# Paced convolution steps and the end of the final RMSNorm, in a two-layer decoder trunk on one core

## The chip, the core and the metric

The kernel runs on one NeuronCore of a Trainium2 chip. Five engines work side by side, each with its own in-order queue: TensorE (PE) multiplies matrices, VectorE (DVE), ScalarE (ACT) and GpSimd (POOL) do elementwise work, and SyncE (SP) issues most of the DMA transfers. They wait for one another by semaphores. The metric is the time of one execution on the device, in microseconds (us).

## The reference

Input x is 512 tokens of 1024 channels, float32; the output has the same shape. There are two layers and a final norm:

```python
h = h + conformer_conv(rmsnorm(h), ...)    # layer A
h = h + swiglu_ffn(rmsnorm(h), ...)
k, v = split(rmsnorm(h, norm_kv) @ w_kv)   # once
h = h + banded_sink_attention(rmsnorm(h) @ w_q, k, v, ...) @ w_o   # layer B
h = h + swiglu_ffn(rmsnorm(h), ...)
out = rmsnorm(h, norm_final)

def conformer_conv(x, ...):
    a = glu(x @ w_pw1 + b_pw1)
    y = causal depthwise conv of a, width 31, + b_dw
    y = silu(layernorm(y))                  # over the channels
    return y @ w_pw2 + b_pw2

def swiglu_ffn(x, w_up, w_down):            # width 2816
    gate, up = split(x @ w_up)
    return (silu(gate) * up) @ w_down
```

rmsnorm(x, g) is x * rsqrt(mean(x*x) + 1e-6) * g, the mean over the channels.

## The kernel before

**Layout.** Everything is transposed: channels lie on the 128 partitions, tokens on the free axis. h is eight tiles of 128 x 512. Where it helps, tokens are worked in two halves of 256 (HALF[0], HALF[1]); h0 and h1, and fa and fb, are objects of the first and the second half.

**Products in three parts.** Most products go through mm3: weight and activation are each split into a high and a low part, and PE computes high by high (L262), weight-high by activation-low (L263) and weight-low by activation-high (L264). The first half's second pointwise product (pw2) is the exception, with one plain matmul (L260). Weights come as a stream of 128 x 1024 chunks in a fixed plan. SP loads them (L187) up to six chunks ahead; up to three chunks ahead ACT casts the high part (L203) and DVE subtracts it from the raw chunk for the low part (L204). `get` hands out the next chunk, and is the clock of all pacing.

**The background convolution.** The depthwise convolution of the first half, h0, is done before its pw2. That of the second half, h1, is a generator of 85 steps, 20 of which are taken early; the other 65 are recorded between the weight chunks of the first half's pw2 (8 chunks), FFN up and FFN down. `job(second, points...)` paces them: at each `get`, `pace` takes steps until as many are done as `due_at` gives by straight lines between the points (chunk, steps done), and behind the last point all the rest. One step works on two channel tiles: per tile one DVE multiply-add (L611), and on average about one product on ACT (L603), which POOL adds up (L604), through a ring of eight `pr` buffers. After each of the four pairs of tiles come its squares (DVE L638, ACT L640) and, on PE with a matrix of ones, its sums (L649). After the last pair follow the LayerNorm's scales: ACT copies the sums (L655), PE turns them (L658), DVE computes mean and variance (L660 to L665), POOL takes a power (L671), ACT makes diagonals (L676), PE spreads them (L680). Then, per channel tile, DVE subtracts and multiplies (L692, L693), ACT applies silu (L694), and the result is split for the second half's pw2 (ACT L386, DVE L387). That pw2 starts when the first half's FFN is over.

**The first half's rows.** As pw2 of the first half yields its eight row tiles, DVE adds each to h (L731). ACT then scales it and casts the high part of the FFN's input (L382), DVE makes the low part (L383), ACT squares (L336) and DVE adds the squares up (L340). The FFN's first matmuls need these parts.

**The end.** The last FFN down product is worked by halves, class Fin: fa, then fb. For each half: `rows` adds PE's result to h (DVE L1047), squares it (ACT L1051) and adds squares (POOL L1053); of fb only the first five tiles are added on POOL. PE turns squares into sums per token with tiny matmuls (`total`, L1039): for fb, in the order tile 5, tile 6, the run of five, tile 7. `sums` computes the mean (`ms`, DVE L1070), the power -1/2 (`rs`, POOL L1072) and a diagonal from it (`diag`, DVE L1074); `spread` broadcasts it with PE (L1084, for fb also into a second bank, L1088, copied by ACT, L1093). The final products are h times the gain times this scale: six tiles of each half on DVE (`out_dve`, L1106, stored by SP, L1096), and two on POOL (`out_pool`, L1100) from tiles that ACT has multiplied by the gain (L1079), stored by SP for fa and by ACT for fb. `fill(n)` places n of fa's DVE products among fb's last steps.

**What sets the order.** The code is recorded once, by tiles; a scheduler then places each engine's instructions by its own estimate of when they can run. `tc.issue_after(x)` keeps what is recorded inside it behind x. So the place of an instruction in an engine's queue need not be the place at which it was recorded.

The last chunks of the kernel, as recorded:

```python
    for n, (kp, g) in enumerate(steps):
        fb.down(kp, g)
        if n == 1:
            fa.sums()
        elif n == 2:
            fb.rows(0)
            fa.spread()
        elif n == 3:
            fb.rows(1, fill)
```

Of the kernel before, what the change touches and what calls it, by code (L numbers as in the profile page):

```python
# [21 lines left out]
KT = D // P  # L22
# [127 lines left out]
def hybrid_trunk(ctx: ExitStack, tc: tile.TileContext, xT, W, prm_in, wdw_in, sinks, relb, onehot, outT):  # L150
    nc = tc.nc
# [10 lines left out]
    def uid(s):  # L162
        ctr[0] += 1
        return f"{s}{ctr[0]}"

    def bank():
        return ps.tile([P, 512], F32, tag="bank", name=uid("bank"))
# [4 lines left out]
    def temp():  # L172
        return tmp.tile([P, 512], F32, tag="tmp", name=uid("tmp"))
# [35 lines left out]
    def job(gen, *points):  # L209

        jobs.append([gen, points, 0])
# [54 lines left out]
    class Act:  # L266
        def __init__(self, n, w=512):
            self.per = 2048 // w
            self.q = [tuple(quads.tile([P, self.per, w], F32R, tag="quad", name=uid("quad")) for _ in range(2))
                      for _ in range(-(-n // self.per))]  # L270
# [51 lines left out]
    def col(name, i):  # L322
        c = PARAM_COLS[name] + i
        return prm[:, c:c + 1]


    class Rms:
# [44 lines left out]
        def spread(self):  # L372
            self.step1()
            pb = bank()[:, 0:self.w]
            self.spread_mm = nc.tensor.matmul(pb, ones_m, self.diag, start=True, stop=True).ins  # L375
            return pb
# [171 lines left out]
    with tc.tile_pool(name="conv", bufs=2) as cv:  # L548
# [29 lines left out]
        class Half:  # L578
# [64 lines left out]
            def sums(self, p):  # L643
                if self.st is None:
                    self.st = bank()
                for e in range(2):
                    ct = 2 * p + e
                    for f, t in enumerate((self.y[:, ct, :], self.sq[e])):
                        mm = nc.tensor.matmul(self.st[:, f * W2:(f + 1) * W2], ones_m, t,  # L649
                                              start=ct == 0 and f == 0, stop=ct == KT - 1 and f == 1)  # L650
                return mm.ins
# [30 lines left out]
            def rows(self, split_z):  # L682
                pb = self.pb
                if split_z:
                    zz = Act(KT, W2)
                    self.z = [zz[i] for i in range(KT)]
                else:
                    zz = quads.tile([P, KT, W2], F32, tag="quad", name=uid("z"))
                    self.z = [zz[:, i, :] for i in range(KT)]
                for i in range(KT):  # L690
                    t = temp()[:, 0:W2] if split_z else self.z[i]
                    nc.vector.tensor_sub(t, self.y[:, i, :], pb[:, 0:W2])  # L692
                    nc.vector.tensor_mul(t, t, pb[:, W2:2 * W2])  # L693
                    self.silu = nc.scalar.activation(t, t, AF.Silu, scale=col("lng", i), bias=col("lnb", i)).ins  # L694
                    if split_z:
                        split(self.z[i], t)
                    yield
# [84 lines left out]
        done, early, late = 0, 0, None  # L782
        for at_, (hf, ct) in enumerate(projs):
# [3 lines left out]
            with tc.issue_after(spread) if at_ == 13 else nullcontext():  # L787
                proj = Pw1(hf, ct, mid=(lambda: h0.sums(3)) if at_ == 11 else None)
# [14 lines left out]
            if at_ == 10:  # L803
                h1 = Half(1, h0.last)
                second = h1.background()
# [15 lines left out]
            late.gate()  # L821
        h1.after = [h0.silu]
        base = seen[0]
        job(second, (base, 0), (base + 8, 20), (base + 36, h1.n_steps - early))
        x0 = {"ffn0": Act(KT)}
        bc0 = new_bc()
        n0 = Next(("ffn0",), x0, bc0, HALF[0], nc.vector)
# [15 lines left out]
    base = seen[0]  # L843
# [15 lines left out]
    if True:  # L859
# [20 lines left out]
        for half in range(2):  # L880
# [7 lines left out]
            if half == 0:  # L888
                rs_bc = rms.step2()
                rs = rms.rs  # L890
                for m in range(2):
                    t = temp()
# [4 lines left out]
        for n in range(4):  # L897
            t = temp()
# [100 lines left out]
        for part in range(2):  # L999
            for g in range(2):  # L1000
# [4 lines left out]
                for m in range(4):  # L1005
                    i = g * 4 + m
# [13 lines left out]
    class Fin:  # L1020
        def __init__(self, hf):
            self.hf, self.tok = hf, HALF[hf]
            self.banks, self.hg = [bank() for _ in range(4)], []
            self.n_pool = 2

        def down(self, kp, g):
            whi, wlo = get("down", 1, kp, g)
# [14 lines left out]
        def rows(self, g, other=lambda n, ins: None):  # L1042

            n_add = 5 if self.hf else KT
            for i in range(g * 4, g * 4 + 4):
                t = h[i][:, self.tok]
                add = nc.vector.tensor_add(t, self.banks[i // 2][:, (i % 2) * 256:(i % 2) * 256 + 256], t)  # L1047
                if i == KT - 1:
                    other(2, add.ins)
                sq = res.tile([P, 256], F32, tag="sq", name=uid("sq"), bufs=5)  # L1050
                self.squared = nc.scalar.square(sq, t).ins  # L1051
                if 0 < i < n_add:
                    nc.gpsimd.tensor_add(sq, self.acc, sq)  # L1053
                if i < n_add:
                    self.run = self.acc = sq
                if not self.hf or i < n_add:
                    continue
                if i == n_add:
                    self.st = bank()
                self.total(sq, i == n_add, i == KT - 1)  # L1060
                if i == KT - 2:
                    self.total(self.run, False, False)

        def sums(self, other=lambda n, ins: None):
            if not self.hf:
                self.st = bank()
                self.total(self.acc, True, True)
            st = self.st
            ms = small.tile([P, 4], F32, tag="ms", name=uid("ms"))
            other(2, nc.vector.tensor_scalar(ms[:, 0:2], st[:, 0:2], 1.0 / D, EPS, op0=ALU.mult, op1=ALU.add).ins)  # L1070
            rs = small.tile([P, 4], F32, tag="rs", name=uid("rs"))
            nc.gpsimd.tensor_tensor(rs[:, 0:2], ms[:, 0:2], mhalf[:, 0:2], op=ALU.pow)  # L1072
            self.diag = temp()[:, 0:256]
            other(2, nc.vector.tensor_mul(self.diag.rearrange("p (n q) -> p n q", n=2),  # L1074
                                          ident.unsqueeze(1).to_broadcast([P, 2, P]),
                                          rs[:, 0:2].unsqueeze(2).to_broadcast([P, 2, P])).ins)
            for i in range(self.n_pool):
                t = res.tile([P, 256], F32, tag="res", name=uid("res"))
                nc.scalar.mul(t, h[i][:, self.tok], col("fin", i))  # L1079
                self.hg.append(t)  # L1080

        def spread(self):
            self.pb = bank()[:, 0:256]
            nc.tensor.matmul(self.pb, ones_m, self.diag, start=True, stop=True)  # L1084
            if self.hf:

                pb = bank()[:, 0:256]
                nc.tensor.matmul(pb, ones_m, self.diag, start=True, stop=True)  # L1088
                self.copy(pb)

        def copy(self, pb):
            self.bc = temp()[:, 0:256]
            nc.scalar.copy(self.bc, pb)  # L1093

        def store(self, i, t, q=nc.sync):
            q.dma_start(outT[i][:, self.tok], t)  # L1096
# [1 line left out]
        def out_pool(self):  # L1098
            for i, t in enumerate(self.hg):
                nc.gpsimd.tensor_mul(t, t, self.bc)  # L1100
                self.store(i, t, nc.scalar if self.hf else nc.sync)

        def out_dve(self):
            for i in range(self.n_pool, KT):
# [3 lines left out]
                self.store(i, t)  # L1108
                yield

    res = ctx.enter_context(tc.tile_pool(name="res", bufs=8))
    steps = [(kp, g) for kp in range(*LAST) for g in range(2)]
    fa = Fin(0)
    for kp, g in steps:
# [3 lines left out]
    fb = Fin(1)  # L1118
# [7 lines left out]
    for n, (kp, g) in enumerate(steps):  # L1126
# [5 lines left out]
            fa.spread()  # L1132
        elif n == 3:
            fb.rows(1, fill)
    with tc.issue_after(fb.squared):
        fa.copy(fa.pb)
    fa.out_pool()
    fb.sums(fill)
    fb.spread()
    for _ in fb.out_dve():  # L1140
# [28 lines left out]
```

## Time and profile before

| | us |
|---|---|
| median of three runs | 1115.81 |
| lowest, highest | 1115.38, 1116.58 |
| profiled execution, its own time | 1115.77 |
| its span in the profile | 1114.0 |
| PE busy in the span | 1098.9 |
| DVE busy | 662.3 |
| ACT busy | 502.6 |
| POOL busy | 322.1 |
| mean granted PE clock | 0.993 of full speed |

The profile has one execution; its times count from the start of its span. Most views are lists: a timeline row is start, duration, engine, line of the kernel, operation, output<-inputs, shape, and "xN" where N like instructions are merged into one row; in brackets stands how long the engine stood idle ahead of it, and what ended that. A row by stretches has the busy time of PE, PE's weight loads, DVE, ACT and POOL in the stretch (each with its number of instructions), then PE's granted clock (1.00 is full speed), the busy share of the DMA engines, and GB/s. The ends of matmuls are modelled, so merged PE rows overlap their neighbours somewhat.

### The profile page before, as it was taken

What the parts mean: (1) busy time and instruction counts of PE and PEld (TensorE: products, weight loads), DVE (VectorE), ACT (ScalarE), POOL (GpSimd) and SP (SyncE); (2) the same over time, 40 slices, a digit from 0 to 9 for tenths busy, and PEclk for the clock granted to TensorE, in tenths of its full rate; (3) what the DMA queues carried; (4) which work ended last, traced back from release to release, by engine and by line L of the source; (5) the groups of instructions that cost most, each with busy time, mean ns of one, the idle gap of its engine ahead of it and who ended that gap; (6) DMA issues with size and microseconds to landing.
All of it is one profiled execution on the core that took longest, in us unless ns stands there. A gap on an engine that the chain in (4) does not pass through costs nothing.

```text
span 1114.0 us, 15803 instructions
## 1 busy us (share of the span) xinstructions
PE 1098.9 (99%) x5994; PEld 955.7 (86%) x5994; DVE 662.3 (59%) x1074; ACT 502.6 (45%) x891; POOL 322.1 (29%) x420
## 2 busy tenths in 40 slices
PE   9999998999999999999999999999999999999997
PEld 8888898999999888888888788888888888888886
DVE  4999999977665454443575686683444333444455
ACT  4786787765543232232343574553322211332233
POOL 4999699700100021110230332241111100110014
PEclk9999998999999999999999999999999999999998
DMA  9227044576655423332322201023233333323332
GB/s 362 100 31 84 25 168 136 183 247 190 189 174 184 135 95 101 105 97 95 95 95 87 75 29 48 30 95 95 95 95 95 97 102 103 96 95 95 95 95 77
DMA packets 40857, 125.00 MB, mean 112 GB/s; under 512 B 4395, under 2 KB 12748, under 8 KB 40780
## 3 DMA queue, kind: packets, MB, share of 16 engines
q1 hardware_dynamic: 40204, 123.55, 36.2%
q8 instruction: 47, 0.77, 0.3%
q10 hardware_dynamic: 576, 0.44, 0.1%
q14 instruction: 30, 0.25, 0.1%
HBM read 118.73 MB, written 5.24 MB: 111 GB/s over the span
## 4 chain that ended last, share of the span: by engine, by line
PE 90%; DVE 5%; ACT 2%; issue 1%; POOL 1%; DMA 0%; SPq 0%; POOLq 0%; DVEq 0%; ACTq 0%
PE bank L263 26%; PE bank L262 26%; PE bank L264 26%; PE bank L562 8%; PE bank L928 1%; DVE quad L383 1%; PE bank L649 1%; ACT pr L603 1%; DVE bank L611 1%; PE bank L950 1%; DVE wlo L204 1%; DMA h<-in_xT_dram 0%; DVE sc L931 0%; PE bank L375 0%; DVE ptl L954 0%
## 5 line engine op out<-in xcount | busy, mean ns | idle before, releaser
L263 PE MATMUL bank<-quad,whi 128*128 128x512 f32 (+1 forms) x1536 | 535.2, 349 | 3.8 <-DVE quad L383 3.7
L262 PE MATMUL bank<-quad,whi 128*128 128x512 f32 (+1 forms) x1536 | 534.8, 350 | 0.5 <-ACT quad L968 0.5
L264 PE MATMUL bank<-quad,wlo 128*128 128x512 f32 (+1 forms) x1536 | 535.1, 348 | 0.0
L204 DVE TENSOR_TENSOR wlo<-raw,whi 128x1024 fp32r<-128x1024 f32 x194 | 262.5, 1354 | 322.4 <-ACT whi L203 312.3
L203 ACT CAST whi<-raw 128x1024 fp32r<-128x1024 f32 x194 | 203.3, 1049 | 360.0 <-PE bank L263 319.3
L263 PEld LDWEIGHTS bank<-quad,whi 128*128 128x128 f32 x1536 | 292.0, 190 | 40.9 <-DVE quad L383 5.0
L262 PEld LDWEIGHTS bank<-quad,whi 128*128 128x128 f32 x1536 | 291.7, 190 | 38.5 <-ACT quad L968 0.9
L264 PEld LDWEIGHTS bank<-quad,wlo 128*128 128x128 f32 x1536 | 292.1, 190 | 36.8 <-issue 0.2
L472 POOL TENSOR_TENSOR tmp<-tmp,tmp 128x512 f32<-128x512 f32 x34 | 48.4, 1425 | 486.7 <-DVE tmp L471 473.1
L604 POOL TENSOR_TENSOR pr<-pr,pr 128x256 f32<-128x256 f32 x208 | 161.6, 825 | 11.0 <-ACT pr L603 11.0
L611 DVE SCALAR_TENSOR_TENSOR bank<-apad,wdw,bank 128x256 f32<-128x256 f32 x248 | 113.2, 485 | 3.6
L562 PE MATMUL bank<-quad,w 128*128 128x256 f32 x512 | 114.2, 382 | 0.6 <-DMA w<-in_W_dram 0.5
L562 PEld LDWEIGHTS bank<-quad,w 128*128 128x128 f32 x512 | 97.4, 191 | 15.4 <-DVE quad L537 1.7
L603 ACT ACTIVATE pr<-apad,wdw 128x256 f32<-128x256 f32 x208 | 99.0, 503 | 20.8 <-POOL pr L604 18.1
L340 POOL TENSOR_TENSOR tmp<-tmp,tmp 128x256 f32<-128x256 f32 (+1 forms) x35 | 38.8, 1109 | 138.6 <-ACT tmp L336 109.1
L470 ACT ACTIVATE tmp<-tmp 128x512 f32<-128x512 f32 x34 | 21.4, 632 | 92.9 <-DVE tmp L469 92.9
L942 POOL TENSOR_SCALAR sc<-sc,sm 128x256 f32<-128x256 f32 (+1 forms) x64 | 30.0, 489 | 79.4 <-DVE sm L940 79.4
L386 ACT CAST quad<-tmp 128x512 fp32r<-128x512 f32 (+1 forms) x50 | 29.1, 586 | 30.4 <-POOL tmp L472 26.6
L471 DVE TENSOR_TENSOR tmp<-bank,rsbc 128x512 f32<-128x512 f32 x34 | 23.5, 691 | 32.4 <-PE bank L264 32.4
L383 DVE SCALAR_TENSOR_TENSOR quad<-h,prm,quad 128x512 fp32r<-128x512 f32 (+1 forms) x40 | 39.5, 1020 | 0.5 <-ACT quad L382 0.4
L938 ACT ACTIVATE sc<-sc,m 128x257 f32<-128x257 f32 (+1 forms) x64 | 30.3, 476 | 15.4 <-DVE m L931 13.7
L387 DVE TENSOR_TENSOR quad<-tmp,quad 128x512 fp32r<-128x512 f32 (+1 forms) x50 | 32.8, 661 | 2.5 <-ACT quad L386 2.5
(140 smaller groups left out, 747.0 us busy)
## 6 DMA issues: line engine op xcount, KB each, us to landing
raw<-in_W_dram SPq DMA_DIRECT2D x202, 512.0 KB, 3.5
w<-in_W_dram SPq DMA_DIRECT2D x15, 512.0 KB, 9.7
fd<-fs SPq DMA_DIRECT2D x1, 3072.0 KB, 33.8
h<-in_xT_dram SPq DMA_DIRECT2D x8, 256.0 KB, 5.9
bias<-fd SPq DMA_DIRECT2D x8, 256.0 KB, 5.5
out_dram<-res SPq DMA_DIRECT2D x14, 128.0 KB, 1.8
w<-in_W_dram SPq DMA_DIRECT2D x2, 256.0 KB, 4.1
out_dram<-res ACTq DMA_DIRECT2D x2, 128.0 KB, 2.7
```

What stands on the lines that cost most here:

```text
L203: nc.scalar.copy(hi, r)
L204: lo_engine[0].tensor_sub(lo, r, f32(hi))
L262: nc.tensor.matmul(out, w[0], x[0], start=start, stop=False)
L263: nc.tensor.matmul(out, w[0], x[1], start=False, stop=False)
L264: nc.tensor.matmul(out, w[1], x[0], start=False, stop=stop)
L340: self.eng.tensor_add(sq, self.acc, sq)
L383: nc.vector.scalar_tensor_tensor(dst[1], src, g, f32(dst[0]), op0=ALU.mult, op1=ALU.subtract)
L472: nc.gpsimd.tensor_mul(t2, t1, t2)
L562: mm = nc.tensor.matmul(self.pb[:, w * W2:(w + 1) * W2], w1[ct][:, w, k, :], x[k] if x else xg[k][:, tok], start=k == 0, stop=k == KT - 1)
L603: on_act = nc.scalar.mul(pr, a[:, j:j + W2], tap(j))
L604: on_pool = nc.gpsimd.tensor_add(pr, acc, pr)
L611: on_dve = nc.vector.scalar_tensor_tensor(yt if i == nd - 1 else c, src, tap(i), c if i else self.shift, op0=ALU.mult, op1=ALU.add)
```

## The change

Two places are edited.

- **Pacing.** The points of h1's background convolution are new: 17 steps done at chunk 6, 20 at chunk 11, 47 at chunk 27 and all 65 at chunk 36. Before, they were 20 at chunk 8 and all at chunk 36.
- **End.** `n_pool` is 0 for fa, so all eight of fa's products go to DVE; fa has no pre-scaled tiles, no copy of its scale and no POOL products. `fill` places three products at each of its places, not two. In `rows`, the total of the run of five tiles is recorded ahead of that of tile 6. The ring `res` has 16 buffers, not eight.

```diff
--- before.py
+++ after.py
@@ -821,7 +821,7 @@
             late.gate()
         h1.after = [h0.silu]
         base = seen[0]
-        job(second, (base, 0), (base + 8, 20), (base + 36, h1.n_steps - early))
+        job(second, (base, 0), (base + 6, 17), (base + 11, 20), (base + 27, 47), (base + 36, h1.n_steps - early))
         x0 = {"ffn0": Act(KT)}
         bc0 = new_bc()
         n0 = Next(("ffn0",), x0, bc0, HALF[0], nc.vector)
@@ -1021,7 +1021,7 @@
         def __init__(self, hf):
             self.hf, self.tok = hf, HALF[hf]
             self.banks, self.hg = [bank() for _ in range(4)], []
-            self.n_pool = 2
+            self.n_pool = 2 * hf
 
         def down(self, kp, g):
             whi, wlo = get("down", 1, kp, g)
@@ -1046,9 +1046,9 @@
                 t = h[i][:, self.tok]
                 add = nc.vector.tensor_add(t, self.banks[i // 2][:, (i % 2) * 256:(i % 2) * 256 + 256], t)
                 if i == KT - 1:
-                    other(2, add.ins)
+                    other(3, add.ins)
                 sq = res.tile([P, 256], F32, tag="sq", name=uid("sq"), bufs=5)
-                self.squared = nc.scalar.square(sq, t).ins
+                nc.scalar.square(sq, t)
                 if 0 < i < n_add:
                     nc.gpsimd.tensor_add(sq, self.acc, sq)
                 if i < n_add:
@@ -1057,9 +1057,9 @@
                     continue
                 if i == n_add:
                     self.st = bank()
-                self.total(sq, i == n_add, i == KT - 1)
                 if i == KT - 2:
                     self.total(self.run, False, False)
+                self.total(sq, i == n_add, i == KT - 1)
 
         def sums(self, other=lambda n, ins: None):
             if not self.hf:
@@ -1071,7 +1071,7 @@
             rs = small.tile([P, 4], F32, tag="rs", name=uid("rs"))
             nc.gpsimd.tensor_tensor(rs[:, 0:2], ms[:, 0:2], mhalf[:, 0:2], op=ALU.pow)
             self.diag = temp()[:, 0:256]
-            other(2, nc.vector.tensor_mul(self.diag.rearrange("p (n q) -> p n q", n=2),
+            other(3, nc.vector.tensor_mul(self.diag.rearrange("p (n q) -> p n q", n=2),
                                           ident.unsqueeze(1).to_broadcast([P, 2, P]),
                                           rs[:, 0:2].unsqueeze(2).to_broadcast([P, 2, P])).ins)
             for i in range(self.n_pool):
@@ -1086,11 +1086,8 @@
 
                 pb = bank()[:, 0:256]
                 nc.tensor.matmul(pb, ones_m, self.diag, start=True, stop=True)
-                self.copy(pb)
-
-        def copy(self, pb):
-            self.bc = temp()[:, 0:256]
-            nc.scalar.copy(self.bc, pb)
+                self.bc = temp()[:, 0:256]
+                nc.scalar.copy(self.bc, pb)
 
         def store(self, i, t, q=nc.sync):
             q.dma_start(outT[i][:, self.tok], t)
@@ -1098,7 +1095,7 @@
         def out_pool(self):
             for i, t in enumerate(self.hg):
                 nc.gpsimd.tensor_mul(t, t, self.bc)
-                self.store(i, t, nc.scalar if self.hf else nc.sync)
+                self.store(i, t, nc.scalar)
 
         def out_dve(self):
             for i in range(self.n_pool, KT):
@@ -1108,7 +1105,7 @@
                 self.store(i, t)
                 yield
 
-    res = ctx.enter_context(tc.tile_pool(name="res", bufs=8))
+    res = ctx.enter_context(tc.tile_pool(name="res", bufs=16))
     steps = [(kp, g) for kp in range(*LAST) for g in range(2)]
     fa = Fin(0)
     for kp, g in steps:
@@ -1132,9 +1129,6 @@
             fa.spread()
         elif n == 3:
             fb.rows(1, fill)
-    with tc.issue_after(fb.squared):
-        fa.copy(fa.pb)
-    fa.out_pool()
     fb.sums(fill)
     fb.spread()
     for _ in fb.out_dve():
```

## The prediction

> **What bounds the kernel now.** I read the page's head first, then the busy time of each engine by stretches, then the timelines of the two places where PE waits.
>
> ```profile
> span 1114.0 us, 15803 instructions
> ```
> ```profile
> 160.00:175.00 15.00, 12.03 (x77) 11.18 (x76) 14.90 (x20) 13.91 (x31) 15.00 (x17) 0.85 0.56 194
> 175.00:300.00 125.00, 125.00 (x1017) 124.05 (x1017) 101.05 (x145) 79.39 (x131) 48.84 (x52) 0.99 0.62 193
> ```
> PE is the bound: it works without a break from 175 to 300 (125.00 of 125), where the first half's FFN runs, as it does nearly everywhere else. An edit can gain only where PE waits or is throttled: between 160 and 175 (12.03 of 15 us busy, clock 0.85) and behind the last weight. In the stretch between, it can only lose.
>
> The first place, by the timelines of PE, DVE, POOL and ACT (start, duration, instruction, in brackets what it waited for) and the clock by stretches:
>
> ```profile
> 169.16 0.39 PE L263 MATMUL bank<-quad,whi 128*128 128x256 f32 x1 [1.88 <-DVE quad L383]
> ...
> 170.90 0.58 PE L263 MATMUL bank<-quad,whi 128*128 128x256 f32 x1 [0.99 <-DVE quad L383]
> ```
> ```profile
> 150.09 0.55 DVE L383 SCALAR_TENSOR_TENSOR quad<-h,prm,quad 128x256 fp32r<-128x256 f32 x1
> ...
> 168.16 0.94 DVE L383 SCALAR_TENSOR_TENSOR quad<-h,prm,quad 128x256 fp32r<-128x256 f32 x1
> 169.03 0.95 DVE L340 TENSOR_TENSOR tmp<-tmp,tmp 128x256 f32<-128x256 f32 x1
> 169.90 1.82 DVE L383 SCALAR_TENSOR_TENSOR quad<-h,prm,quad 128x256 fp32r<-128x256 f32 x2
> 171.64 0.95 DVE L340 TENSOR_TENSOR tmp<-tmp,tmp 128x256 f32<-128x256 f32 x1
> 172.51 0.95 DVE L383 SCALAR_TENSOR_TENSOR quad<-h,prm,quad 128x256 fp32r<-128x256 f32 x1
> 173.39 1.82 DVE L340 TENSOR_TENSOR tmp<-tmp,tmp 128x256 f32<-128x256 f32 x2
> 175.13 3.42 DVE L204 TENSOR_TENSOR wlo<-raw,whi 128x1024 fp32r<-128x1024 f32 x2
> ```
> ```profile
> 156.55 26.37 POOL L604 TENSOR_TENSOR pr<-pr,pr 128x256 f32<-128x256 f32 x26
> ```
> ```profile
> 169.73 0.51 ACT L603 ACTIVATE pr<-apad,wdw 128x256 f32<-128x256 f32 x1 [0.34 <-POOL pr L604]
> 170.15 1.03 ACT L203 CAST whi<-raw 128x1024 fp32r<-128x1024 f32 x1
> ```
> ```profile
> 170.00:171.00 1.00, 0.10 (x1) 0.10 (x1) 1.00 (x2) 1.00 (x2) 1.00 (x2) 0.77 0.97 389
> 171.00:177.00 6.00, 5.91 (x26) 5.61 (x27) 5.90 (x7) 4.26 (x9) 6.00 (x7) 0.50 0.03 11
> 177.00:178.00 1.00, 1.00 (x9) 1.00 (x9) 1.00 (x1) 0.49 (x1) 1.00 (x2) 0.82 0.29 33
> ```
> PE runs out of low parts (L383) 1.88 us before 169.16 and is fed one row at a time until the last of them ends at 173.46 (172.51 + 0.95). DVE stands ahead of it without a gap: low parts, sums of squares, then two weight splits. Not one convolution product (L611) lies between 168.16 and the end of the two L204 at 178.55. The wait costs a second time: the clock falls to 0.50 for 6.8 us (0.23/0.5 in the first row, 6, and 0.18/0.5 in the last), as if PE stood still for 3.4.
>
> **The change, part by part.**
>
> *Pacing.* Steps due by weight chunk: before 2.5 a chunk to 8, then 45 over 28 chunks, 1.61 each; after 2.83 to 6, 0.6 to 11, 1.69 to 27, 2.0 to 36. At chunk 11 the change owes 20 where before had 20 + 3 x 1.61 = 24.8. The end point is the same. Recording order isn't yet engine order: a scheduler places the instructions, so I compared the queues of the two built programs.
> - DVE's queue is the same, instruction by instruction, up to and with the two L204 at 175.13. The first products that move later are five L611 behind these. What ends the stall, L383 at 172.51, keeps all its predecessors. Gain: 0.
> - ACT: two L603 (one of them the 169.73 row) move behind the cast L203 at 170.15. Its L204 stands behind DVE's L340 at 173.39 anyway. POOL doesn't starve: 169.73 waited for POOL to free a product buffer, of which there are eight, so it has several times 26.37/26 = 1.01 us of work in store. POOL's order is kept but for one small L354. Gain 0, cost 0.
> - PE: the four L649 of the second pair of tiles, which stood ahead of the FFN's first matmul, move 48 matmuls later, directly in front of the L263 that waits. PE has the same work done when it reaches that wait. Sum 0.
>
> So the pacing, as I read the queues, leaves the stall as it is. What it puts off falls into the stretch where PE is full:
>
> ```profile
> 225.02 0.59 PE L649 MATMUL bank<-y,ones_m 128*128 128x256 f32 x2
> ...
> 229.62 0.95 PE L658 MATMUL bank<-ident,tmp 128*128 128x1 f32 x8
> ```
> ```profile
> 226.94 0.59 ACT L655 COPY tmp<-bank 128x512 f32<-128x512 f32 x1 [0.75 <-PE bank L649]
> ```
> ```profile
> 256.69 0.75 DVE L387 TENSOR_TENSOR quad<-tmp,quad 128x256 fp32r<-128x256 f32 x2
> ```
> ```profile
> 263.11 1.05 ACT L203 CAST whi<-raw 128x1024 fp32r<-128x1024 f32 x1 [1.83 <-PE bank L263]
> 265.99 1.05 ACT L203 CAST whi<-raw 128x1024 fp32r<-128x1024 f32 x1 [1.83 <-PE bank L263]
> ```
> One chunk is 2.88 us (265.99 - 263.11), 24 matmuls of 0.12. The last pair's L649 move 48 matmuls later (225.02 to about 230.8), L658 50 (to about 235.6), the spread L680 behind it 48, with its inputs moved alike. Their inputs come later too. Squares of the last pair: two chunks' worth of products later on DVE, estimate 228.4, 2.4 us before PE. The ACT copy for L658: L649 + the 1.92 between 225.02 and 226.94, about 232.8, and 0.59; with a cast of 1.05 ahead of it, 234.2 to 234.4. That leaves some 1.3 us. (Before, it was 229.62 - 227.53, 2.1.) The last z row (256.69 + 0.75 = 257.44) comes some 8 us later, 265.8, for a second-half pw2 that needs it some 4 us later. All margins are positive, so cost 0; the smallest is what I trust least. Freed DVE time between 178 and 205 feeds weight splits that PE doesn't wait for: 0.
>
> *The end.* PE, DVE and POOL around and behind the last weight:
>
> ```profile
> 1101.17 0.59 PE L1084 MATMUL bank<-tmp,ones_m 128*128 128x256 f32 x2
> ...
> 1102.35 1.50 PE L1039 MATMUL bank<-ones_c,sq 128*128 128x1 f32 x12 [0.26 <-ACT sq L1051]
> 1105.97 1.22 PE L1084 MATMUL bank<-tmp,ones_m 128*128 128x256 f32 x2 [2.12 <-DVE tmp L1074]
> ```
> ```profile
> 1102.04 0.86 DVE L1106 SCALAR_TENSOR_TENSOR res<-h,prm,bank 128x256 f32<-128x256 f32 x2
> 1103.89 0.16 DVE L1070 TENSOR_SCALAR ms<-bank 128x2 f32<-128x2 f32 x1 [0.99 <-PE bank L1039]
> 1103.97 0.86 DVE L1106 SCALAR_TENSOR_TENSOR res<-h,prm,bank 128x256 f32<-128x256 f32 x2
> 1105.49 0.43 DVE L1074 TENSOR_TENSOR tmp<-ident,rs 128x256 f32<-128x256 f32 x1 [0.66 <-POOL rs L1072]
> 1105.83 0.87 DVE L1106 SCALAR_TENSOR_TENSOR res<-h,prm,bank 128x256 f32<-128x256 f32 x2
> 1107.23 2.44 DVE L1106 SCALAR_TENSOR_TENSOR res<-h,prm,bank 128x256 f32<-128x256 f32 x6 [0.53 <-PE bank L1084]
> ```
> ```profile
> 1103.38 1.41 POOL L1100 TENSOR_TENSOR res<-res,tmp 128x256 f32<-128x256 f32 x2 [1.40 <-ACT tmp L1093]
> 1104.75 0.71 POOL L1072 TENSOR_TENSOR rs<-ms,mhalf 128x2 f32<-128x2 f32 x1
> ```
> The chain is: last h add, its square, the totals, ms, the power on POOL, the diagonal on DVE, the spread L1084, six products, their stores. Step by step:
> 1. The first half's L1084 now stands ahead of PE's last L264, so the last add comes later by what its two records take, 0.59 less the overlap with the next: 0.43.
> 2. Behind the last square stood three totals, 12 records in 1.50, 0.125 each; the five tiles' total now stands between the last two squares, so two remain: -0.50. With +0.43, ms ends at about 1104.0 (1103.89 + 0.16 - 0.07).
> 3. POOL finished ms's power late: ms was there at 1104.05, POOL had its two products until 1104.79 (1103.38 + 1.41). All first-half products are now DVE's, so the power starts where ms ends: -0.7, that is 1104.05 to 1104.75.
> 4. DVE: three products (1.2 us) fill the time before ms; two fill the wait for the power, and end at about 1104.84; the diagonal starts at 1104.86 in place of 1105.49: **-0.63**. The last three products stand between diagonal and spread: 1104.86 + 0.34 + 1.2 = 1106.4, while the spread that DVE needs next comes at 1107.23 - 0.63 = 1106.6. Hidden, by 0.2 us; without that cover they cost up to 1.2.
> 5. SP still issues 14 stores, since the first half's two POOL stores move over to DVE's list; ACT keeps the second half's two; the last six stores keep their pace and go with the products. ACT loses two pre-scales and a copy, none on the chain.
>
> The clock at this place could change the price of the spread: 1.22 us at 1105.97 against 0.59 at 1101.17. If it came before the drop, up to 0.6 more. I take 0, as 0.63 is close to what lies between. The bounds for the end are -1.4 (diagonal, full clock, both together) and +0.5 (L1084's 0.43, nothing gained).
>
> **Sum.** 0 (stall) + 0 (middle) - 0.6 (end). The profiled execution took 1115.77, of which 1114.0 is span; the median of the runs is 1115.81, so nothing to correct: 1115.77 - 0.6, about 1115.1.
>
> [...] The three runs of before lie 1115.38 to 1116.58 apart. [...]
>
> **The rivals.**
> - *Faster: the stall shrinks after all.* For it: L383 and L340, back to back, take 0.95 each in the stall, as long as one POOL add beside them (1.01). Where they have more room they are short: L383 0.55 at 150.09, and the like of L340, the subtraction at 256.69 with POOL idle, 0.37. If POOL had fewer adds to do just then, four L383 would lose 0.39 each and two L340 0.5: 2.6 us, and half of the dip's 3.4, 1.7, if one stretch of low clock fell away with it. Against it: POOL's row has no gap from 156.55 to 182.9, and its order is kept. Time 1115.1 - 2.6 or - 4.3: 1112.5 or 1110.8, about 1112. [...]
> - *Slower: a moved step stalls PE.* L658 waits for ACT's copy with 1.3 us to spare. If casts and FFN work ahead of it on ACT take 1.5 us more than that, PE, full there, waits 1.5 us, and as in the stall a stretch at half clock follows, half a dip, 1.7: 1115.1 + 3.2, about 1118.3. It decides from a delay of 1.3 us. For it: the margin is the sum of moved queues. Against: PE has not one wait from 175 to 300 before, and the inputs move with it.
> - *No gain at the end.* The 0.2 us of step 4 isn't there, or the diagonal waits behind the products: 1115.8.
>
> **How the numbers follow.** Likeliest, stall unchanged and 0.6 off the end: 0.55. No gain at the end: 0.13. Faster rival: 0.17. Slower rival: 0.15. About 0.2% (2.2 us) is what a measurement can tell from no change: the first two fall within it, 0.68; faster 0.17; slower 0.15. Range: the likeliest alone has 1114.0 to 1116.6 (the end's bounds, -1.4 and +0.5 against 1115.77, and 0.4 below and 0.3 above for the spread of the runs); the faster rival takes it down to 1112.0; above, 1117.2 adds half of the 1.2 between the runs of before to 1116.6. Outside lie the slower rival and a little of the faster one's far end.
>
> **What would show it.** The stall's L383 rows at 168.16 to 172.51 the same within 0.1 us, with PE's waits of 1.9 and 1.0; no PE wait from 175 to 300; at the end eight records of L1039 behind the last square, the power right behind ms, the diagonal 1.4 us behind ms's start or less, no POOL product for the first half. It is wrong if the rows of DVE in the stall are shorter, if PE shows a wait at L658 or L680, or if the last six products start no earlier behind PE's last L264 than the 5.9 us here.

## The result, and the profile after

| | before | changed |
|---|---|---|
| median of 16 runs, us | 1115.93 | 1118.38 |
| lowest to highest | 1115.01 to 1117.23 | 1117.10 to 1120.81 |
| profiled execution, its span | 1115.77, 1114.0 | 1118.0, 1116.2 |

The ratio is 1.0021, with a 95% interval of 1.0014 to 1.0027: slower by 2.4 us, where 0.7 less was forecast. The loss is small, but clear of the noise.

The stretches of the changed kernel that answer to the two shown of before (columns as there), and what PE waited for from 175 to 300:

```profile
160.00:175.00 15.00, 11.91 (x86) 10.87 (x85) 14.78 (x21) 14.30 (x30) 15.00 (x16) 1.00 0.54 199
175.00:300.00 125.00, 121.70 (x990) 119.98 (x989) 100.83 (x144) 79.07 (x130) 48.70 (x54) 1.00 0.59 190
```
```profile
PE bank L375 <- ACT tmp L362: 1.5, 1, 1.5
PE bank L264 <- DVE wlo L204: 1.3, 1, 1.3
PE bank L262 <- ACT whi L203: 0.4, 1, 0.4
```
Two things stand out. The clock is 1.00 from 160 to 300; the low-clock stretch behind the stall is gone. And PE, which had 125.00 busy of 125, now has 121.70: it waits 1.5 us for the spread of the FFN's scale, L375, and 1.8 us for a split weight chunk. PE got faster in one place and lost more in the next.

The stall itself, in the timelines of PE and DVE:

```profile
169.38 0.38 PE L263 MATMUL bank<-quad,whi 128*128 128x256 f32 x1 [1.19 <-DVE quad L383]
171.12 0.39 PE L263 MATMUL bank<-quad,whi 128*128 128x256 f32 x1 [0.78 <-DVE quad L383]
173.74 0.39 PE L263 MATMUL bank<-quad,whi 128*128 128x256 f32 x1 [1.12 <-DVE quad L383]
```
```profile
168.38 0.94 DVE L383 SCALAR_TENSOR_TENSOR quad<-h,prm,quad 128x256 fp32r<-128x256 f32 x1
...
172.74 0.95 DVE L383 SCALAR_TENSOR_TENSOR quad<-h,prm,quad 128x256 fp32r<-128x256 f32 x1
```
DVE's rows are those of before, 0.22 us later, with the same durations. PE's wait is cut into three.

The place where the time goes, PE and ACT of the changed kernel, and then PE, ACT and DVE of before:

```profile
204.05 0.39 PE L262 MATMUL bank<-quad,whi 128*128 128x256 f32 x1 [0.42 <-ACT whi L203]
...
205.88 0.39 PE L264 MATMUL bank<-quad,wlo 128*128 128x256 f32 x1 [1.34 <-DVE wlo L204]
...
208.62 0.59 PE L649 MATMUL bank<-y,ones_m 128*128 128x256 f32 x2
```
```profile
195.13 1.30 ACT L603 ACTIVATE pr<-apad,wdw 128x256 f32<-128x256 f32 x3
197.55 0.51 ACT L603 ACTIVATE pr<-apad,wdw 128x256 f32<-128x256 f32 x1 [1.11 <-POOL pr L604]
197.96 1.03 ACT L203 CAST whi<-raw 128x1024 fp32r<-128x1024 f32 x1
...
202.97 1.03 ACT L203 CAST whi<-raw 128x1024 fp32r<-128x1024 f32 x1
```
```profile
197.38 0.59 PE L649 MATMUL bank<-y,ones_m 128*128 128x256 f32 x2
```
```profile
194.91 1.31 ACT L603 ACTIVATE pr<-apad,wdw 128x256 f32<-128x256 f32 x3
196.12 1.03 ACT L203 CAST whi<-raw 128x1024 fp32r<-128x1024 f32 x1
...
201.41 1.03 ACT L203 CAST whi<-raw 128x1024 fp32r<-128x1024 f32 x1
```
```profile
202.48 1.79 DVE L204 TENSOR_TENSOR wlo<-raw,whi 128x1024 fp32r<-128x1024 f32 x1 [0.58 <-ACT whi L203]
```
Before, the sums of the third pair of tiles (four L649, 1.73 us) stood at 197.4, and PE came to the weight chunk near 205 some 0.8 us after it was ready (the last row above ends at 204.27; PE came at 205.10, with the 291st three-part matmul). Now they stand at 208.6. PE comes to the chunk early, waits 1.76 us in all, and has the 1.73 us of sums still to do.

That can be followed by counting PE's three-part matmuls (L262, L263, L264; 4872 in each kernel, in the same order) in the traces. Start of the n-th before, and how much later it starts in other runs, us (e1, e2, e3, e9 and e10 are experiments below):

```
n        before   changed    e1     e2     e3     e9    e10
1        161.06    -0.96  -1.64  -0.10  -1.05  -1.64  +1.02
241      198.92    -1.41  -1.77  -1.00  -1.60  -2.15  -1.43
301      206.30    +0.88  +1.18  -0.75  +0.69  +0.16  +0.36
346      211.70    +2.60  +3.43  -0.31  +1.14  +0.58  +2.08
4001     923.56    +2.61  +3.45  -0.29  +4.73  +0.61  +2.10
```
In the changed kernel, e1, e3 and e9 the 1.73 us of the second pair's sums come only behind n = 1, so by the start of its work the changed kernel is 0.78 us later (-0.96 + 1.73), e3 0.68 and e1 and e9 0.09. Such differences of the start, up to 1.0 us, are there from 35 us on, with the same instructions ahead of them, so they come from the run and not from the change. With the start taken off, what is lost up to n = 346 is 1.82 us in the changed kernel (2.60 - 0.78), 0.49 in e9, 1.06 in e10, 0.46 in e3 and -0.21 in e2. It is settled between n = 241 and n = 346, in 13 us; in the 712 us behind that nothing is added but in e3.

### The profile page after: what moved, and what is told of

It is laid out like the page before. It is cut to its first block, busy times and chain, and to the rows that moved or that the text cites. A ratio compares the mean times of both kernels' runs of the same rounds, so it can differ in the third digit from the quotient of the medians.

```text
span 1116.2 us, 15795 instructions
## 1 busy us (share of the span) xinstructions
PE 1097.6 (98%) x5994; PEld 954.2 (85%) x5994; DVE 663.9 (59%) x1076; ACT 501.6 (45%) x888; POOL 320.5 (29%) x418
## 2 busy tenths in 40 slices
DMA packets 40857, 125.00 MB, mean 112 GB/s; under 512 B 4395, under 2 KB 12748, under 8 KB 40780
## 4 chain that ended last, share of the span: by engine, by line
PE 87%; issue 4%; DVE 3%; ACT 3%; POOL 2%; DMA 0%; POOLq 0%; SPq 0%; ACTq 0%
PE bank L262 25%; PE bank L263 25%; PE bank L264 25%; PE bank L562 9%; POOL pr L604 2%; PE bank L928 1%; ACT pr L603 1%; PE bank L649 1%; PE bank L950 1%; DVE quad L383 1%; DVE bank L611 0%; ACT whi L203 0%; DVE wlo L204 0%; DMA w<-in_W_dram 0%; DVE sc L931 0%
## 5 line engine op out<-in xcount | busy, mean ns | idle before, releaser
L263 PE MATMUL bank<-quad,whi 128*128 128x512 f32 (+1 forms) x1536 | 534.2, 348 | 4.0 <-DVE quad L383 4.0
L264 PE MATMUL bank<-quad,wlo 128*128 128x512 f32 (+1 forms) x1536 | 534.2, 348 | 1.3 <-DVE wlo L204 1.3
L262 PE MATMUL bank<-quad,whi 128*128 128x512 f32 (+1 forms) x1536 | 533.9, 349 | 0.9 <-ACT quad L968 0.5
L263 PEld LDWEIGHTS bank<-quad,whi 128*128 128x128 f32 x1536 | 290.8, 189 | 41.7 <-DVE quad L383 5.1
L262 PEld LDWEIGHTS bank<-quad,whi 128*128 128x128 f32 x1536 | 290.6, 189 | 38.8 <-ACT quad L968 0.9
L264 PEld LDWEIGHTS bank<-quad,wlo 128*128 128x128 f32 x1536 | 290.8, 189 | 38.3 <-DVE wlo L204 1.7
L383 DVE SCALAR_TENSOR_TENSOR quad<-h,prm,quad 128x512 fp32r<-128x512 f32 (+1 forms) x40 | 39.5, 1021 | 0.5 <-ACT quad L382 0.4
```

The lines of the kernel that those rows point to most:

```text
L262: nc.tensor.matmul(out, w[0], x[0], start=start, stop=False)
L263: nc.tensor.matmul(out, w[0], x[1], start=False, stop=False)
L264: nc.tensor.matmul(out, w[1], x[0], start=False, stop=stop)
L383: nc.vector.scalar_tensor_tensor(dst[1], src, g, f32(dst[0]), op0=ALU.mult, op1=ALU.subtract)
```

## The experiments

**The two halves of the change, alone.** The first puts the new points into the kernel before, the second the old points into the changed kernel:

```diff
-job(second, (base, 0), (base + 8, 20), (base + 36, h1.n_steps - early))
+job(second, (base, 0), (base + 6, 17), (base + 11, 20), (base + 27, 47), (base + 36, h1.n_steps - early))
```

> The kernel before with the new pacing points alone; its end is unchanged. Theory A (the new pacing puts two waits on PE, 1.5 us at the spread L375 and 1.8 us at a weight chunk near 204, and the new end gives about 0.5 back): 1115.9 + 2.9, about 1118.8, with both waits in its profile. Rival B (the pacing is neutral, as predicted, and the new end costs): 1115.9 and no PE wait between 175 and 300.

> The changed kernel with the old pacing points, so the new end alone. Theory A: 1115.9 - 0.5, about 1115.4, and no PE wait between 175 and 300. Rival B: about 1118.4, the whole loss.

e1 took 1118.46 beside 1116.28 of before, ratio 1.0020 (1.0012 to 1.0029). e2 took 1115.86, ratio 0.9996 (0.9987 to 1.0004). The loss is the pacing's; the new end costs nothing, and its gain can't be told from none by the times. In its profile e1 has the waits at the weight chunk (1.4 and 0.3 us), but none at L375: here the low clock behind the stall was there (0.69 from 167 to 178, about 6.8 us at 0.50), PE came to L375 later, and lost the time at the same chunk all the same. A second low-clock stretch follows there (0.89 from 200 to 215, about 3.3 us at 0.50), and the loss by the count is 3.34 us, 1.5 more than in the changed kernel.

**Which of the points.**

```diff
e3: +job(second, (base, 0), (base + 6, 17), (base + 11, 20), (base + 36, h1.n_steps - early))
e4: +job(second, (base, 0), (base + 8, 20), (base + 27, 47), (base + 36, h1.n_steps - early))
```

> The kernel before with the points 17 at chunk 6 and 20 at chunk 11 and from there a straight line to the end. Up to chunk 11 the queues are those of the change. Theory A: the same two waits, 1118.5 within 0.6. Rival C (the points at 27 and 36, which crowd the last steps, are what costs): 1115.9 within 0.5.

> The kernel before with its own first point, 20 at chunk 8, and the new 47 at chunk 27. L375 stands six matmuls earlier on PE than before, not thirteen. Theory A: at most 0.6 us of wait at L375, 1115.9 to 1116.5. Rival C: 1118.5.

e3 took 1119.77, ratio 1.0031 (1.0019 to 1.0043), e4 1116.10, ratio 0.9998 (0.9989 to 1.0006). By themselves the early points cost, and the late ones don't. But e3 isn't the changed kernel's loss: it loses more than expected, and at another place. PE at L658, and the clock of that stretch:

```profile
232.74 1.05 PE L658 MATMUL bank<-ident,tmp 128*128 128x1 f32 x8 [1.73 <-ACT tmp L655]
```
```profile
230.00:240.00 10.00, 8.28 (x53) 7.72 (x53) 4.76 (x9) 5.13 (x10) 1.14 (x4) 0.83 0.90 284
```
A wait of 1.73 us and a stretch at half clock behind it, here with nothing downstream to hide it: 3.6 us between n = 346 and n = 4001. Near 205, where the changed kernel loses, e3 loses little. PE of e3:

```profile
203.29 0.59 PE L649 MATMUL bank<-y,ones_m 128*128 128x256 f32 x2
...
205.71 0.39 PE L264 MATMUL bank<-quad,wlo 128*128 128x256 f32 x1 [0.30 <-DVE wlo L204]
```
Its third pair's sums still stand in front of the weight chunk. In e4 they do too, at 199.5. Only both sets of points together put them behind it.

**Is POOL the engine that is behind?** ACT's product at 197.55 waits for POOL, and a cast stands behind it. e5 gives POOL less to do, e6 gives ACT more buffers:

```diff
e5: -N_POOL = ((13, 13, 12, 12), (17, 15, 15, 15))
e5: +N_POOL = ((13, 13, 12, 12), (17, 15, 13, 15))
e6: -pr = cv.tile([P, W2], F32, tag="pr", name=uid("pr"), bufs=8)
e6: +pr = cv.tile([P, W2], F32, tag="pr", name=uid("pr"), bufs=12)
```

> The changed kernel with 13 of 31 taps on POOL, not 15, for the third pair of tiles: four POOL adds and four ACT products fewer between 186 and 213, four DVE multiply-adds more. PE's queue is the changed kernel's up to the spread L375 (six matmuls later). Theory A (POOL is the engine that is behind, ACT's products wait for its buffers, and the weight casts behind them come late): the wait at a weight chunk near 204 falls from 1.8 us to under 0.5, and the time to 1116.5 within 0.7. Rival D (PE is simply early, ACT's queue is too full by itself): the wait stays, 1118.4.

> The changed kernel with twelve product buffers between ACT and POOL, not eight. Theory A: casts no longer stand behind a product that waits for POOL; no wait near 204, 1116.3 within 0.7. Rival D: 1118.4.

Both miss. e6 took 1119.09, ratio 1.0027 (1.0018 to 1.0036): the waits only move.

```profile
PE bank L263 <- DVE quad L383: 2.7, 4, 0.8
PE bank L264 <- DVE wlo L204: 1.6, 3, 0.7
PE bank L262 <- ACT whi L203: 1.1, 1, 1.1
PE bank L375 <- ACT tmp L362: 0.7, 1, 0.7
```
e5 took 1125.85, ratio 1.0083 (1.0069 to 1.0098). Four multiply-adds more go to DVE, and two steps more fall into the same chunks. In its profile, which is of its slowest run (1128.11), PE waits 3.3 us for low parts of weights between 162 and 206 and 1.1 for a high part, 2.4 of the two together near 204, and the LayerNorm's spread comes too late for PE, with low clock behind it:

```profile
255.19 2.08 PE L680 MATMUL bank<-tmp,ones_m 128*128 128x512 f32 x2 [4.01 <-ACT tmp L676]
```
```profile
250.00:262.00 12.00, 7.99 (x45) 6.76 (x45) 8.30 (x23) 6.12 (x13) 1.62 (x1) 0.72 0.66 224
```
Each of the two edits also shifts the queues around it, so they don't show that POOL is innocent. They show only that these two ways of relieving it don't help; whether POOL is why the casts come late stays open.

**Does each wait count?** e7 records the spread L375 one weight chunk later; `thirds` collects the L264 of mm3:

```diff
-            nc.scalar.copy(self.bc[:, self.tok], self.spread())
+            with tc.issue_after(thirds[-1]) if self.w == 256 and thirds else nullcontext():
+                pb = self.spread()
+            nc.scalar.copy(self.bc[:, self.tok], pb)
...
-                    if half == 0 and which == 1:
+                    if (half, which) == ((1, 0) if w == 256 and tok.start == 0 and layer == 0 else (0, 1)):
```

> The changed kernel with the first half's spread L375 recorded one weight chunk later, which puts it 17 matmuls later on PE. Theory A (the supply of split weights sets when PE goes on near 204): the wait of 1.5 us at L375 goes and comes back at the next weight chunk, 1118.0 within 0.6. Rival E (each wait counts by itself): 1118.4 - 1.5, about 1116.9.

e7 took 1117.42, ratio 1.0012 (1.0003 to 1.0021), half way between the two expectations, so the time doesn't decide. The profile does: the wait at L375 is gone, and a wait of 1.98 us at 195.1, on ACT's copy of that same scale, has taken its place, with a low-clock stretch beside it (0.92 from 178 to 200, about 3.5 us at 0.50). PE then has no wait at the chunk near 205. By the count, e7 begins 0.32 us later than before (-1.41 + 1.73) and stands at +2.15 at n = 346: 1.83 lost in between, as the changed kernel lost 1.82. At n = 301, just behind the chunk, both are as far behind before when the start is taken off: 0.11 us in e7, 0.10 in the changed kernel. So the loss doesn't hang on the wait at L375, though the stretch at low clock keeps e7 from being a clean test.

**The sums alone.** Here the third pair's L649 are moved, by the step at which they are due, and nothing else of note (the other queues change by a few swaps between 204 and 223):

```diff
-                    due += [(4, lambda p=p: self.squares(p)), (8, lambda p=p: self.sums(p))]
e9, in the changed kernel:
+                    due += [(4, lambda p=p: self.squares(p)), (5 if p == 2 else 8, lambda p=p: self.sums(p))]
e10, in the kernel before:
+                    due += [(4, lambda p=p: self.squares(p)), (12 if p == 2 else 8, lambda p=p: self.sums(p))]
```

> The changed kernel with the sums of the third pair (four L649, 1.73 us of PE) due at the fifth step of the next pair, not the eighth. They stand 48 matmuls earlier on PE, ahead of the wait near 204 and not behind it; the queues of the other engines are all but the same. Theory G (PE reaches the weight chunk near 204 too early and waits 1.76 us there; the sums that stood ahead of it before now come behind and are paid again): PE fills the wait with them, 1118.4 - 1.7, about 1116.7, wait under 0.3 us. Rival H (the new casts' order on ACT costs by itself): 1118.4 within 0.5.

> The kernel before with the same sums due at the twelfth step, so that they stand where the change puts them, and nothing else of the change. Theory G: a new wait of about 0.9 us near 204, or up to 1.7, and the time 1116.2 + 0.9 to 1.7, about 1117.2. Rival H: 1116.2 within 0.4, no wait.

e9 took 1116.26, ratio 1.0003 (0.9994 to 1.0012), 2.1 us less than the changed kernel. e10 took 1117.10, ratio 1.0013 (1.0004 to 1.0021). In time both go as theory G has it; the wait left in e9 is 0.52 us, where under 0.3 was expected. PE of e9, then of e10:

```profile
199.65 0.59 PE L649 MATMUL bank<-y,ones_m 128*128 128x256 f32 x2
...
205.17 0.39 PE L264 MATMUL bank<-quad,wlo 128*128 128x256 f32 x1 [0.52 <-DVE wlo L204]
```
```profile
205.37 0.39 PE L264 MATMUL bank<-quad,wlo 128*128 128x256 f32 x1 [1.33 <-DVE wlo L204]
208.10 0.59 PE L649 MATMUL bank<-y,ones_m 128*128 128x256 f32 x2
```
e9 has the sums in front of the wait, and the wait is 0.52; it keeps the 1.5 us wait at L375, the late cast and all the rest of the change, and takes the time of before, with the 0.3 to 0.4 us that the new end gives (below) in it. e10 is the kernel before with the sums behind, and has the wait of the changed kernel. In the table, the 1.72 us between n = 301 and n = 346, the same in the changed kernel and in e10, are the sums being done there.

The sums aren't the whole loss. The low part of the chunk near 205 on DVE, in the changed kernel, e9 and e10 (before it starts at 202.48):

```profile
204.03 1.80 DVE L204 TENSOR_TENSOR wlo<-raw,whi 128x1024 fp32r<-128x1024 f32 x1 [0.53 <-ACT whi L203]
```
```profile
203.30 1.81 DVE L204 TENSOR_TENSOR wlo<-raw,whi 128x1024 fp32r<-128x1024 f32 x1 [0.53 <-ACT whi L203]
```
```profile
203.51 1.80 DVE L204 TENSOR_TENSOR wlo<-raw,whi 128x1024 fp32r<-128x1024 f32 x1 [0.58 <-ACT whi L203]
```
With the start of each run taken off, e10 has the chunk when before has it (203.51 - 1.02 = 202.49), and the changed kernel and e9 have it 0.7 to 0.8 us later (203.25, 203.21). So two things add up. The sums behind the chunk cost 1.06 by themselves (e10), close to their 1.73 less the 0.8 for which the chunk had been ready. With the sums back in front and the chunk still late, 0.49 is left (e9). In the changed kernel, where the later chunk has used up the 0.8, they cost 1.82 together. That is an account of these numbers; no run moves the chunk alone.

**The end.** e8 puts the total of the five tiles back behind tile 6 in e2; e11 holds the first half's spread behind the last weight, e12 its diagonal behind the second half's first adds as well:

```diff
e8:
-                if i == KT - 2:
-                    self.total(self.run, False, False)
                 self.total(sq, i == n_add, i == KT - 1)
+                if i == KT - 2:
+                    self.total(self.run, False, False)
e11:
             fb.rows(0)
-            fa.spread()
         elif n == 3:
+            with tc.issue_after(thirds[-1]):
+                fa.spread()
             fb.rows(1, fill)
e12, and as e11:
-        if n == 1:
-            fa.sums()
...
             fb.rows(0)
...
+            with tc.issue_after(fb.last_add):
+                fa.sums()
```

> The new end alone, old pacing, with the total of five tiles recorded behind that of tile 6 again. By the prediction its place was worth 0.5 us behind the last square: 1115.9 + 0.5, 1116.4. Rival F (the moved total waits for POOL's last add and gains nothing): 1115.9 within 0.3, and the mean's start no later behind PE's last weight than in the new end alone.

> The new end alone, old pacing, with the first half's spread L1084 held behind PE's last weight matmul, where the kernel before has it. By the prediction its place ahead costs 0.43 us: 1115.9 - 0.4, about 1115.5, the last h add 0.4 us nearer to the last weight. Rival: the first half's products then wait for the spread and DVE gives the gain back: 1115.9.

> As the run before, and the first half's diagonal and its sums on DVE recorded behind the second half's first four h adds, so that POOL's adds and the total of five tiles aren't late. The wait of PE for POOL's last add (0.5 us in the new end) goes: another 0.3 less, 1115.2. Rival: what is gained there is lost in the first half's chain, 1115.5 or more.

Their medians and ratios are 1115.57, 0.9998 (0.9989 to 1.0007); 1116.04, 1.0007 (0.9999 to 1.0016); 1115.93, 1.0000 (0.9992 to 1.0009). None can be told from before or from e2; 1116.4 was expected of e8 by the prediction, 1115.5 of e11 and 1115.2 of e12. The profiles tell more. Start of the second half's diagonal, less what PE was ahead or behind at its 4861st three-part matmul: before 1105.49, e2 1105.18, e8 1105.30, e11 1105.13, e12 1105.17, the changed kernel 1105.12. So the place of the total is worth 0.1 us, that of the spread 0.05, and the whole new end 0.3 to 0.4, each from one profile. No run here is faster than before by more than its interval.

## Why the prediction was wrong

- *The stall keeps its length: right.* DVE's rows from 168 to 175 are the same, and the waits for L383 sum to 3.1 us against 2.9.
- *The second price of 3.4 us for the stall, by the clock: wrong in its meaning.* The low clock behind the stall lasted 6.8 us in the profiles of before, e1 and e8 (0.69 from 167 to 178), 3.4 in e2, e4 and e10 (PE's matmuls start 0.21 apart, not 0.12, from 171.8 to 175.2, 170.9 to 174.3 and 172.3 to 175.7), and wasn't there in the changed kernel and e3 (1.00) nor in e9 (0.12 apart behind the waits). It didn't decide the time: e2 with 3.4 and e8 with 6.8 stand 0.31 and 0.23 us ahead of before at n = 346. e2 is 1.00 ahead at n = 241 and gives 0.69 of it back at the weight chunks near 205 to 211. By this the 1.7 us that the faster rival took off for a shorter dip would have been worth nearly nothing here. That a dip could come in halves, on which both rivals' 1.7 rests, was the author's estimate: the profile of before has only a whole one, of 6.8; the 3.4 of e2, e4 and e10 came later. In e3, with no such wait behind, the dip does cost (3.6 us for a wait of 1.73 and half of 3.4).
- *"0 (middle)", from "it works without a break from 175 to 300": the step that failed.* The prediction saw that in this stretch an edit can only lose, and put the loss at 0, as nothing that it looked at came late for PE. But busy PE was read as PE with time of its own. The split weights were only a little ahead of it: the chunk near 205 had been ready for 0.8 us when PE came, so PE couldn't use more than that of the 1.73 us of work that the change took away in front of it, and had all 1.73 still to do behind it. The prediction went through the sums of the second and of the last pair, and the steps behind them, and left out the third pair's, which move furthest, by 72 matmuls. It also left out that the chunk itself could come later. In place of 0 the middle lost 1.82 us by the count: the sums are 1.06 of it by themselves (e10), and 1.33 of it goes when they alone are put back (1.82 - 0.49, e9). The L375 that the change moves 13 matmuls forward was left out too; it makes a wait of 1.5, which by e1 and e9 isn't what the loss hangs on.
- *"ACT: gain 0, cost 0": off by what lies later.* Up to 175 it holds. At 197.55 a product that waits 1.11 us for POOL stands in front of a cast, and the casts come 1.5 us later than before (202.97 against 201.41), of which 0.8 is this run's start. The 0.7 to 0.8 that is left is the later chunk above. That POOL is the reason is likely by these rows, but not shown.
- *L658, L680 and the late z rows at 0: right for the changed kernel* (no wait there), with the margin as thin as said: e3 waits 1.73 at L658, with half a dip behind it, just as the slower rival had it. That rival had the sign, and by luck the size (1118.3 against 1118.38), for another place; its chance of 0.15 was worked out for L658 alone, and moved steps as a class had deserved more.
- *The end at -0.6: right in sign, 0.3 to 0.4 in size.* The power starts right behind ms, and the first half's last products are hidden, as said; the last add, behind L1084, comes 0.43 us later, as said. What was mis-sized is step 2, -0.50 for two totals instead of three behind the last square. In PE and POOL of the changed kernel:

```profile
1105.22 1.50 PE L1039 MATMUL bank<-ones_c,sq 128*128 128x1 f32 x12 [0.51 <-POOL sq L1053]
```
```profile
1102.81 2.35 POOL L1053 TENSOR_TENSOR sq<-sq,sq 128x256 f32<-128x256 f32 x3 [1.27 <-ACT sq L1051]
```
All 12 records stand behind a wait, now for POOL's sum of five, which ends at 1105.16: DVE's diagonal of the first half (0.96 us there) has gone in front of the adds that feed it. The step is worth 0.1 (e8), not 0.5.
- *The range, 1112.0 to 1117.2, was too low on the upper side*, as it stopped short of the slower rival.

What stays open: by the profiles the changed kernel loses 1.82 us in the middle and gains 0.3 to 0.4 at the end, some 1.5 in all, and its medians lose 2.4. The sums by themselves are 1.2 by the medians of e10 and 2.1 by e9's against the changed kernel's. The intervals, 0.7 to 1.0 us to either side, hardly tell these apart. In e1 and e7 a low-clock stretch follows a wait between 195 and 206; whether some runs of the changed kernel have one too, and lose more by it, isn't shown.

## What to carry to other kernels

An engine that is busy all the time may still be paced by another: before a piece of its work is called movable at no cost, look how long the next input had been ready when the engine came to it. Here the input had been ready for 0.8 us. Moving 1.73 us of work from in front of that place to behind it cost 1.06, and where the input came later as well, the whole came to 1.82. List every group that a schedule moves on the bounding engine, the far movers first, and in a kernel that is laid out by a scheduler compare the whole queues, not only the part the edit aims at.

## What the runs showed of the hardware

The low-clock stretches of the stall lasted 3.4 us (e2, e4, e10) or 6.8 (before, e1, e8), began anywhere from 169.7 (e8) to 172.3 (e10), and were there in e1 (clock 0.69 from 167 to 178) and missing in the changed kernel (1.00), though both have the same work up to the end. What sets when one begins, and how long it lasts, isn't shown here.

In e5 one L383 on DVE, of 128x256, took 5.47 us, where the next two took 0.47 and 0.57. Beside it stand the last 5.2 us of a run of 18 POOL adds at 0.69 us each, and it ended 0.3 us behind them, when POOL had run out of products (an idle time of 2.46 stands ahead of POOL's next row). DVE and POOL of e5:

```profile
147.14 5.47 DVE L383 SCALAR_TENSOR_TENSOR quad<-h,prm,quad 128x256 fp32r<-128x256 f32 x1 [0.42 <-ACT quad L382]
```
```profile
139.93 12.40 POOL L604 TENSOR_TENSOR pr<-pr,pr 128x256 f32<-128x256 f32 x18 [9.56 <-ACT pr L603]
154.78 0.73 POOL L604 TENSOR_TENSOR pr<-pr,pr 128x256 f32<-128x256 f32 x1 [2.46 <-ACT pr L603]
```
In the stall of before, where the two kinds run side by side, they took 0.95 and 1.0 each. Why it was so long here wasn't tried.
